# An encoder block on one core: one square moved ahead, K's low parts on GpSimd, and gate weight forms in another order

## The chip, the cores and the metric

The kernel runs on one core of one Trainium2 chip. The time is device microseconds of one execution, first to last, the lower the better. The engines are named as in the profile: PE is TensorE (matrix products), ACT is ScalarE, DVE is VectorE, POOL is GpSimd, SP is SyncE, which here issues the DMAs.

## The reference

One layer of an encoder on 1024 tokens of width 1024, all in float32:

```python
u = rms_norm(x, norm1_g)
proj = u @ w_in                       # 1024 x (3*512 + 3*512 + 2*1024)
q, k, v, cb, cc, ch, ga, gb = split(proj)
q = rms_norm(q.reshape(B, S, 8, 64), q_norm_g)
k = rms_norm(k.reshape(B, S, 8, 64), k_norm_g)
y_a = neighbourhood_attention(q, k, v, rpb) @ w_attn_branch
y_b = short_gated_conv(cb, cc, ch, conv_w) @ w_conv_branch
merged = sigmoid(ga) * y_a + sigmoid(gb) * y_b
x = x + merged @ w_o
h = rms_norm(x, norm2_g) @ w_mlp_in   # 1024 -> 4096
x = x + square(relu(h)) @ w_mlp_out
```

The attention works on a 16 x 64 grid of tokens with a window of 8 rows by 16 columns and a learned bias. The convolution has width 3.

## The kernel before

**High and low parts.** Float32 accuracy comes from 16-bit products. Each operand is scaled by a power of two and split into a high part (its rounding to float16, made by ACT) and a low part (what the rounding left out, made by DVE as value times scale minus high part). A product is three passes: high by high, high by low, low by high (`PASSES`). The scale of a weight matrix is taken from the sum of the squares of its elements: ACT squares piece after piece and adds up each row, DVE adds the pieces (L273) and puts the sum into a column of `ones` (L275), one small product on PE adds over the partitions (`all_sum`, L201), and a few short DVE instructions (L204, L435 to L442, L282) make the scale from it. Only then can ACT make the high parts of the weights (L309) and DVE the low parts (L300).

**Stages.** First the input blocks are normalised, split and transposed, and V is computed (8 blocks of 128 tokens, `v_unit`, 24 products each). Then Q (8 blocks) and K (8 blocks), 24 products each, and behind each block a chain of small steps: ACT squares the products (L747), DVE sums per head (L752), ACT takes the root (L757), DVE inverts it (L763 to L766) and multiplies (L772, and for K by the gains, L774); then ACT makes the high part (L781), DVE the low part (L786), and SP transposes the result by DMA (L793). The high and the low part of block n are put into the queues within the chain of block n + 1 (`qk_chain`). Behind K come the products of the convolution, whose weights are prepared during the K blocks, and then the attention, mixed with the rest of the convolution. Then eight gate groups, the output projection, and the MLP.

**Gates and MLP** use a scheme with seven products instead of eight for a matrix cut in 2 x 2 (`seven`). For the weights of such a group there are seven forms: the four quarters (some of them) and sums of quarters, which GpSimd makes (`gsum`, L1274). `forms_split` makes the high parts (L1294) and low parts (L1290) of the seven forms in four steps. The products of a gate group take the forms in the order 0, 5, 1, 6, 3, 4, 2, as `gate_units` gives it together with `SEVEN`. When certain steps are done, `then` counts two raw weight pieces as used up, and `load_upto` puts the loads of the next pieces into SP's queue.

**Order.** Every engine runs its queue in the order in which the program writes it. Long preparations are Python generators in the list `bg`; each `tick()` runs the first of them up to its next `yield`. During the V stage that generator is `Chunk.prep` of Q's weights: its first four steps are the four squares (L269), the next one the sum L273 and L275; the small product L201 comes once one more group of products has been written. `sform_rows(n)` scales two row blocks of the input on ACT (L491, two instructions), and `sform_sums(n)` forms four sums of them on GpSimd (L498), which the gates use much later.

Of the kernel before, what the change touches and what calls it, by code (L numbers as in the profile page):

```python
# [15 lines left out]
OP = mybir.AluOpType  # L16
# [36 lines left out]
def encoder_block(ctx: ExitStack, tc: tile.TileContext, x, weights, cols, gqk, rel, masks, out):  # L53
    nc = tc.nc
    V, A, G, T, SP = nc.vector, nc.scalar, nc.gpsimd, nc.tensor, nc.sync
# [10 lines left out]
    def bank(tag):  # L66
        return psum.tile([128, 512], F32, name="ps_" + tag, tag=tag, bufs=banks[tag])
# [29 lines left out]
    def at(c, i, n=1):  # L97
        return slice(c.start + i, c.start + i + n)
# [22 lines left out]
    def advance(g):  # L121
        try:
            return next(g) or True
        except StopIteration:
            return False
# [7 lines left out]
    def tick(n=1):  # L133

        for _ in range(n):
            i = 0
            while i < len(bg):
                r = advance(bg[i])
                if not r:
                    bg.pop(i)  # L140
                elif r == WAIT and side[0]:
                    i += 1
                else:
                    break
# [62 lines left out]
    def unit(mms, post=None, steps=0, ticks=0, free=False):  # L207

        for ps, l, r, a, b in mms:
            T.matmul(ps, l, r, start=a, stop=b, skip_group_check=free)  # L210
        for g in list(hooks):
            if not hold[0] and not advance(g):
                hooks.remove(g)
        units[0] += 1
        work[0] += len(mms) * mms[0][0].shape[-1]
        settle()
        if post:
            late.append(post)
        for i in range(max(steps, ticks)):
            if i < steps:  # L220
                step()
            if i < ticks:
                tick()
# [16 lines left out]
    def load_upto(n):  # L240
        while loaded[0] < min(n - held[0], limit[0], len(loads)):
            ch, p = loads[loaded[0]]
            loaded[0] += 1
            t = rawp.tile([128, 1024], F32, name="raw")
            load_into(t[:, :ch.widths[p][0] * ch.widths[p][1]], ch, p)
            ch.raw.append(t)
# [98 lines left out]
    for (kind, j), pieces in plan():  # L345
        ch = chunks[kind, j] = Chunk(kind, [(nk, sum(n for _, n in cs)) for _, _, nk, cs in pieces],
                                     {"A": "wa", "B": "wb"}.get(kind, "ws"), rows.get(kind, lambda j: g1)(j),
                                     j if kind == "V" else None, 9 if kind in "VQKCS" else 0)
# [8 lines left out]
    for q in range(6, 14, 2):  # L357
# [3 lines left out]
    cV, cConv, cA, cB, cO, c1, c2, c2x = ([chunks[k, j] for j in range(n)] for k, n in  # L361
                                              (("V", 2), ("C", 4), ("A", 4), ("B", 4), ("O", 2),
                                               ("1", 16), ("2", 4), ("X", 4)))
# [100 lines left out]
    def group(ps, pairs):  # L464
        return [(ps, l, r, i == 0, i == len(pairs) - 1) for i, (l, r) in enumerate(pairs)]
# [22 lines left out]
    def sform_rows(n):  # L488
        assert n in turned and n + 4 in turned
        for b in (n, n + 4):  # L490
            A.activation(xt[:, b], xt[:, b], AF.Copy, scale=sc[:, at(ys, b)])  # L491

    def sform_sums(n, part=range(4)):
        z = [xt[:, b, c:c + 512] for b in (n, n + 4) for c in (0, 512)]
        for i in part:
            o, a, b, op = ((3, 2, 3, OP.subtract), (2, 0, 2, OP.subtract),
                           (0, 3, 0, OP.subtract), (1, 1, 0, OP.add))[i]
            G.tensor_tensor(z[o], z[a], z[b], op=op)  # L498
# [29 lines left out]
    def v_unit(b, ticks):  # L528
        ps = bank("ds"[ORDER.index(b) % 2])
        order = [(k, p) for k in range(8) for p in PASSES]  # L530
        if b == 2:
            order.sort(key=lambda o: o[1] == HL)

        def post():
            hi, lo = (VT[:, b, s] for s in range(2))
            A.activation(hi, ps, AF.Copy, scale=2.0 ** -20)
            V.scalar_tensor_tensor(lo, ps, 2.0 ** -20, hi, op0=OP.mult, op1=OP.subtract)
        unit(group(ps, [(UT[:, sa, k, b * 128:(b + 1) * 128], vhome[0][:, :, sw, k * 256:(k + 1) * 256])
                        for k, (sa, sw) in order]), post, 0, ticks)
# [154 lines left out]
    settle()  # L694
    tick()
    v_unit(3, 0)
    sform_rows(3)
    sform_sums(3)
    tick(2)
    v_unit(7, 1)  # L700
    for b in 0, 1:
        ln_step(b, 2)
# [27 lines left out]
    todo = [("q", b) for b in ORDER] + [("k", b) for b in range(8)]  # L730
# [52 lines left out]
    def qk_low(n):  # L783
        d = blocks[n]
        t, q = d["t"], d["q4"]
        V.tensor_tensor(t[:, :, 1, 0], q[:, :, 0], t[:, :, 0, 0], op=OP.subtract)  # L786
        if d["r"] == 2:
            A.activation(t[:, :, 1, 1], t[:, :, 1, 0], AF.Copy)

# [5 lines left out]
    def qk_chain(n, ps):  # L795
        qk_square(n, ps)
        if n:
            qk_high(n - 1)
        qk_sum(n)
        qk_root(n)  # L800
        if n:
            qk_low(n - 1)
        qk_inverse(n)
        qk_norm(n)
# [57 lines left out]
    for half in range(2):  # L862
        unit(ch_mms(first[half], actU, half, cConv[0], 8, 384, 0), None, 8, 4)
        if half == 0:
            qk_high(15)
            qk_low(15)
            qk_turn(14)
            qk_turn(15)
# [412 lines left out]
    def parts(todo, s, then, pace=False):  # L1281

        prev = None
        for n, it in enumerate(todo + [None]):
            if prev:
                o, w = prev
                if pace:
                    yield from apart(last_low[0], 1)
                    last_low[0] = units[0]
                V.scalar_tensor_tensor(o(1), w, sc[:, s], o(0), op0=OP.mult, op1=OP.subtract)  # L1290
                then(n - 1)
            if it:
                o, w = it
                A.activation(o(0), w, AF.Copy, scale=sc[:, s])  # L1294
            prev = it
            yield

    def forms_split(ch, t, s, P):

        def then(n):  # L1300
            if n == 1 and ch is not c1[0]:
                done[0] += 2
                load_upto(done[0] + 5)
        r = ch.r
        todo = [(0, 1, r[0][:, 0:1]), (1, 3, r[1]), (3, 5, t[:, 0:2]), (5, 7, t[:, 2:4])]
        yield from parts([((lambda i, a=a, b=b: P[:, a:b, i]), w) for a, b, w in todo], s, then)

    def prep_s(n):

        ch = cS[n]  # L1310
        t = w3p.tile([128, 4, 512], F32, name="gsum", bufs=1)
        yield from rows_scaled(ch, g1)
        yield from forms_sum(ch, t, 2 - 0 * (n != 3))
        s, ch.inv = yield from scale_of(ch.sum, 9, 2 + 1*(n != 3), 0)
        hold[0] = True
        while done[0] < ch.first:
            yield WAIT
        ch.P = wsp.tile([128, 7, 2, 512], F16, name="w16_s", tag="ws")
        yield from forms_split(ch, t, s, ch.P)
        ch.split = True  # L1320
        hold[0] = False
# [320 lines left out]
    def prep1(q):  # L1642

        ch = c1[q]
        s, ch.inv = yield from scale_of(ch.sum, 9, 1)
        yield from gate(q)
        P = P1[q] = base2.tile([128, 8, 2, 512], F16, name="w16_1", tag="B")
        yield from forms_split(ch, tsum[q], s, P)
        ready.add(q)
# [712 lines left out]
```

## Time and profile before

| what | value |
|---|---|
| time, median of 3 runs | 1194.14 us (1193.83 to 1194.72) |
| profiled execution, its own time | 1194.58 us |
| its span, first to last instruction | 1192.6 us |
| granted TensorE clock | 1.00 |
| ACT busy in the span | 769.3 us (65%) |
| GpSimd busy in the span | 410.5 us (34%) |
| DMA | 189.61 MB, mean 159 GB/s |

The span is 2.0 us shorter than the execution's own time, which holds a little before the first and after the last instruction. In the timeline a line is a start, a length, an engine, a source line, an operation, output<-inputs, shapes and a count; neighbours of one kind are merged, and what stands in brackets is idle time of the engine before it and the work that ended it. In the waits a line is: who waited, for whom, us in total, times, the longest. In the view by lines, behind the bar, are the busy time, the mean ns of one, and idle time before them. In the view by windows each engine has its busy time and its number of instructions.

### The profile page before, as it was taken

The page shows a single profiled execution, that of the slowest core. Times are in us where ns is not written, and L with a number is a line of the kernel's source. Part 1 is how long each engine was busy: PE and PEld are TensorE (multiplying, and loading weights), DVE is VectorE, ACT ScalarE, POOL GpSimd, SP SyncE. Part 2 cuts the span into 40 slices and gives each one's busy share as a digit, 9 for nine tenths or more (in the row PEclk, how much of TensorE's full clock was granted, in tenths as well). Part 3 has the DMA queues.
Part 4 walks back from the last instruction along what each step waited for, and adds up shares of the span by engine and source line. Part 5 has one row for each costly group of instructions (what it writes and reads, how often), then busy time and mean ns, then how long its engine had stood idle before and what let it go on. Part 6 is the DMA issues. An engine that isn't in the chain of part 4 may idle for free.

```text
span 1192.6 us, 17069 instructions
## 1 busy us (share of the span) xinstructions
PE 1185.4 (99%) x6291; PEld 581.3 (49%) x6291; DVE 959.0 (80%) x1666; ACT 769.3 (65%) x1192; POOL 410.5 (34%) x284
## 2 busy tenths in 40 slices
PE   9999999999999999999999999999999999999998
PEld 7444445555444444444467445554444444444444
DVE  6788888899678686877886867766748899998998
ACT  7877588787667777436776576666686743646440
POOL 2640011214321212001012475776873431224194
PEclk9999999999999999999999999999999999999999
DMA  9949556776625454243374454533565927235302
GB/s 296 212 154 214 112 127 134 141 153 113 179 103 179 142 177 144 86 154 130 78 164 150 158 177 176 195 130 133 207 255 203 376 74 264 89 141 194 106 36 106
DMA packets 181283, 189.61 MB, mean 159 GB/s; under 512 B 138192, under 2 KB 138704, under 8 KB 177104
## 3 DMA queue, kind: packets, MB, share of 16 engines
q1 hardware_dynamic: 181200, 188.52, 52.4%
q8 instruction: 49, 0.80, 0.3%
q14 instruction: 34, 0.28, 0.1%
HBM read 117.19 MB, written 37.75 MB: 130 GB/s over the span
## 4 chain that ended last, share of the span: by engine, by line
PE 57%; issue 6%; POOL 5%; DMA 3%; DVE 3%; ACT 2%; SPq 0%; POOLq 0%; DVEq 0%; ACTq 0%
PE ps_s L210 21%; PE ps_d L210 20%; PE ps_o L210 15%; DMA hs<-as 3%; POOL tsum L1671 3%; POOL as L1559 2%; PE ps_d L1158 1%; DVE w L1290 1%; DVE as L2009 1%; SPq L1149 0%; ACT raw L1662 0%; DMA raw<-in_weights 0%; PE ps_o L1122 0%; ACT as L1932 0%; DVE w_s L1290 0%
## 5 line engine op out<-in xcount | busy, mean ns | idle before, releaser
L210 PEld LDWEIGHTS <-ops 128*128 128x128 f16 x1356 | 132.5, 98 | 157.3
L210 PEld LDWEIGHTS <-w 128*128 128x128 f16 x1272 | 124.4, 98 | 127.1 <-issue 0.2
L1158 PE MATMUL ps_d<-uT,w_ws 128*128 128x512 f16 x528 | 123.7, 379 | 0.0
L210 PE MATMUL ps_d<-ops 128*128 128x512 f16 (+1 forms) x528 | 119.7, 377 | 0.0
L1559 POOL TENSOR_TENSOR as<-as 128x512 f32<-128x512 f32 x56 | 92.0, 1643 | 74.0 <-ACT as L1934 71.0
L210 PE MATMUL ps_s<-ops 128*128 128x512 f16 (+1 forms) x516 | 117.1, 377 | 0.0
L2186 ACT ACTIVATE ops<-hf,sc 128x2048 f16<-128x2048 f32 x26 | 52.0, 2000 | 86.0 <-PE ps_d L210 37.5
L210 PEld LDWEIGHTS <-w_s 128*128 128x128 f16 x672 | 65.1, 98 | 79.2 <-DVE w_s L1290 1.5
L210 PEld LDWEIGHTS <-uT 128*128 128x128 f16 x528 | 51.4, 98 | 62.4 <-issue 0.6
L1671 POOL TENSOR_TENSOR tsum<-raw 128x512 f32<-128x512 f32 x28 | 40.5, 1462 | 114.4 <-ACT raw L1662 114.4
L1158 PEld LDWEIGHTS <-w_ws 128*128 128x128 f16 x528 | 51.4, 98 | 54.2
L2188 DVE SCALAR_TENSOR_TENSOR ops<-hf,sc,ops 128x2048 f16<-128x2048 f32 x26 | 69.5, 2673 | 3.5 <-ACT ops L2186 3.5
L210 PE MATMUL ps_o<-ops 128*128 128x512 f16 x312 | 71.6, 379 | 0.0
L1274 POOL TENSOR_TENSOR gsum<-raw 128x512 f32<-128x512 f32 x14 | 18.6, 1341 | 125.4 <-ACT raw L1260 100.0
L210 PE MATMUL ps_d<-u2T,w 128*128 128x512 f16 (+1 forms) x276 | 58.2, 360 | 0.0
L1290 DVE SCALAR_TENSOR_TENSOR w<-tsum,sc,w 128x1024 f16<-128x1024 f32 x28 | 46.3, 1661 | 14.5 <-ACT w L1294 14.5
L210 PE MATMUL ps_s<-u2T,w 128*128 128x512 f16 (+1 forms) x252 | 54.0, 364 | 0.0
L1290 DVE SCALAR_TENSOR_TENSOR w<-raw,sc,w 128x1024 f16<-128x1024 f32 (+1 forms) x20 | 28.2, 1417 | 31.7 <-ACT w L1294 31.7
L1932 ACT ACTIVATE as<-as 128x2048 f32<-128x2048 f32 (+1 forms) x18 | 30.9, 1718 | 31.5 <-DVE as L2009 19.3
L1088 ACT ACTIVATE sz<-sz,sc 128x384 f32<-128x384 f32 (+1 forms) x64 | 37.2, 581 | 20.9 <-DVE sc L1079 13.7
L309 ACT ACTIVATE w_ws<-raw,sc 128x512 f16<-128x512 f32 (+1 forms) x64 | 37.2, 655 | 19.6 <-DVE sc L282 19.6
L210 PE MATMUL ps_s<-u2x,w 128*128 128x512 f16 (+1 forms) x228 | 48.5, 362 | 0.0
(434 smaller groups left out, 2691.4 us busy)
## 6 DMA issues: line engine op xcount, KB each, us to landing
raw<-in_weights SPq DMA_DIRECT2D x97, 512.0 KB, 4.5
hs<-as SPq DMA_DIRECT2D x16, 1792.0 KB, 8.4
hf<-hs SPq DMA_DIRECT2D x26, 1024.0 KB, 6.0
w2x<-in_weights SPq DMA_DIRECT2D x16, 512.0 KB, 7.0
raw<-in_weights SPq DMA_DIRECT2D x16, 384.0 KB, 3.5
mL<-in_weights SPq DMA_DIRECT2D x10, 512.0 KB, 5.1
mH<-in_weights SPq DMA_DIRECT2D x9, 512.0 KB, 4.3
xt<-in_x SPq DMA_DIRECT2D x8, 512.0 KB, 7.9
```

The costliest lines, as they stand in the source:

```text
L210: T.matmul(ps, l, r, start=a, stop=b, skip_group_check=free)
L309: A.activation(self.parts[:, 0, f + o:f + o + m], self.raw[p][:, o:o + m], AF.Copy, scale=sc[:, c:c + 1])
L1088: A.activation(z, z, AF.Exp, scale=-1.0, bias=sc[:, d["mx"]], accum_out=sc[:, d["sm"]])
L1158: T.matmul(ps, l, r, start=a, stop=b)
L1274: G.tensor_tensor(t[:, o], a, b, op=OP.add)
L1290: V.scalar_tensor_tensor(o(1), w, sc[:, s], o(0), op0=OP.mult, op1=OP.subtract)
L1559: sub.tensor_tensor(z[o], z[a], z[b], op=op)
L1671: G.tensor_tensor(t[:, o], a, b, op=OP.add)
L1932: A.activation(v[:, 0:4], v[:, 0:4], AF.Relu)
L2009: add, less = (lambda o, a, b, op=op: V.tensor_tensor(o, a, b, op=op) for op in (OP.add, OP.subtract))
L2186: A.activation(P[:, 1, 0], hf, AF.Copy, scale=sc[:, Rs])
L2188: V.scalar_tensor_tensor(P[:, 1, 1], hf, sc[:, Rs], P[:, 1, 0], op0=OP.mult, op1=OP.subtract)
```

## The change

Three edits. The first moves a `tick()` of the V stage ahead of the scaling of two rows, so that the fourth square of Q's weights stands in ACT's queue before the two scalings. The second gives the low parts of K (`r` is 1) to GpSimd; those of Q stay on DVE. The third changes the order of the four steps of `forms_split`, so that the forms come as 0, 5 and 6, 1 and 2, 3 and 4, and lets `then` count the raw pieces after the third step instead of the second.

```diff
@@ -694,9 +694,10 @@
     settle()
     tick()
     v_unit(3, 0)
+    tick()
     sform_rows(3)
     sform_sums(3)
-    tick(2)
+    tick()
     v_unit(7, 1)
@@ -783,7 +784,7 @@
     def qk_low(n):
         d = blocks[n]
         t, q = d["t"], d["q4"]
-        V.tensor_tensor(t[:, :, 1, 0], q[:, :, 0], t[:, :, 0, 0], op=OP.subtract)
+        (V if d["r"] == 2 else G).tensor_tensor(t[:, :, 1, 0], q[:, :, 0], t[:, :, 0, 0], op=OP.subtract)
         if d["r"] == 2:
             A.activation(t[:, :, 1, 1], t[:, :, 1, 0], AF.Copy)
@@ -1298,11 +1299,11 @@
     def forms_split(ch, t, s, P):
 
         def then(n):
-            if n == 1 and ch is not c1[0]:
+            if n == 2 and ch is not c1[0]:
                 done[0] += 2
                 load_upto(done[0] + 5)
         r = ch.r
-        todo = [(0, 1, r[0][:, 0:1]), (1, 3, r[1]), (3, 5, t[:, 0:2]), (5, 7, t[:, 2:4])]
+        todo = [(0, 1, r[0][:, 0:1]), (5, 7, t[:, 2:4]), (1, 3, r[1]), (3, 5, t[:, 0:2])]
         yield from parts([((lambda i, a=a, b=b: P[:, a:b, i]), w) for a, b, w in todo], s, then)
```

## The prediction

> **What bounds it.** I read the page's engine times first, then the waits of PE, then the waits of all engines between 48 and 137 us, then the timeline at the three places that the change touches.
>
> ```profile
> span 1192.6 us, 17069 instructions
> ...
> PE 1185.4 (99%) x6291; PEld 581.3 (49%) x6291; DVE 959.0 (80%) x1666; ACT 769.3 (65%) x1192; POOL 410.5 (34%) x284
> ```
> ```profile
> PE ps_d L210 <- DVE w_s L1290: 0.6, 1, 0.6
> PE ps_o L201 <- DVE ones L275: 0.4, 1, 0.4
> ```
>
> TensorE is busy all but 1192.6 − 1185.4 = 7.2 us, so no edit can win more than a few us. The change aims at just two of the listed waits: 0.4 us for the sum of Q's squares (edit 1) and 0.6 us for a gate group's weight forms (edit 3). It can still lose time without limit, wherever a side chain becomes late enough to stop PE. There is one place where a side chain is already the later of the two, the start of the conv products:
>
> ```profile
> 131.59 5.34 PE L210 MATMUL ps_s<-w_ws,uT 128*128 128x512 f16 x24
> 131.85 0.60 ACT L747 ACTIVATE sq<-ps_d 128x512 f32<-128x512 f32 x1 [2.90 <-PE ps_d L210]
> ...
> 135.91 0.22 DVE L282 TENSOR_SCALAR sc<-sc 128x8 f32<-128x8 f32 x1
> 136.17 4.16 ACT L309 ACTIVATE w_ws<-raw,sc 128x384 f16<-128x384 f32 x8 [2.66 <-DVE sc L282]
> ...
> 136.84 5.57 PE L210 MATMUL ps_o<-uT,w_ws 128*128 128x512 f16 x24
> ...
> 142.25 5.34 PE L210 MATMUL ps_s<-uT,w_ws 128*128 128x512 f16 x24
> ```
>
> The last K product group starts at 131.59. A group of 24 unhindered takes about 5.18 to the next one's start (5.34 less the overlap), so PE is due at 136.77. The conv group starts at 136.84, 0.67 us after ACT begins its weights, and its successor at 142.25 where 142.02 was possible: 0.07 + 0.23 = 0.3 us are lost here, and PE follows the side chain (DVE L282, ACT L309) with no reserve. Is that side chain driven by PE, or does it run by itself?
>
> ```profile
> ACT sq L747 <- PE ps_d L210: 2.9, 1, 2.9
> ...
> ACT sq L747 <- PE ps_d L201: 1.3, 1, 1.3
> ```
>
> These are the only two entries in the waits of 48 to 137 us in which ACT, DVE or Pool waits for PE, and both belong to the last K blocks. So from 48 us until then the Q and K side chain runs by itself, behind PE, and hands on any delay.
>
> **Edit 1, the fourth square first.**
>
> ```profile
> 33.32 0.40 SPq L237 DMA_DIRECT2D raw<-in_weights  x1
> ```
> ```profile
> DMA to landing us min/median/max: 5.2/5.5/5.8
> ```
> ```profile
> 39.21 2.18 ACT L491 ACTIVATE xt<-xt,sc 128x1024 f32<-128x1024 f32 x2
> 41.29 1.04 ACT L269 ACTIVATE w_ws<-raw 128x1024 bf16<-128x1024 f32 x1
> ...
> 42.65 0.75 DVE L275 TENSOR_TENSOR ones<-sc 128x1 bf16<-128x1 f32 x1
> ...
> 43.98 4.04 DVE L456 SCALAR_TENSOR_TENSOR u<-xt,sc,u 128x1024 f16<-128x1024 f32 x2
> ...
> 48.55 0.14 DVE L204 TENSOR_SCALAR sc<-ps_o 128x1 f32<-128x1 f32 x1
> ...
> 49.74 5.01 ACT L309 ACTIVATE w_ws<-raw,sc 128x512 f16<-128x512 f32 x8 [4.27 <-DVE sc L282]
> ```
> ```profile
> 42.12 1.27 POOL L498 TENSOR_TENSOR xt<-xt 128x512 f32<-128x512 f32 x1
> ```
>
> The fourth piece of Q lands by 33.32 + 5.8 = 39.1, so the square can take ACT's place at 39.21 without a wait. The sum in `ones` (L275) is ready about 2 us earlier and PE's 0.4 us goes. The two scalings (L491) then end at 39.21 + 1.04 + 0.1 (accumulator read, an estimate) + 2.18 = 42.5, not 41.4. Pool's sums of those rows began at 42.12, as soon as Pool was free; they now begin at about 42.55, 0.4 us later. Behind them stand DVE's two L456, which take 4.04 us because Pool's sums alternate with them. So L204, and with it Q's weights (L309), move from 48.55 and 49.74 to about 48.95 and 50.15. PE needs these weights only after two more V groups, so it does not see this; the side chain does. Edit 1 by itself: 0.4 us gained on PE at 43 us, 0.4 us lost on the chain that PE meets again at 136 us.
>
> **Edit 2, K's low parts on GpSimd.** One K block's steps, the low part being L786:
>
> ```profile
> 127.93 0.68 DVE L752 TENSOR_REDUCE sc<-sq 128x8 f32<-128x512 f32 x1
> 128.05 0.63 ACT L781 ACTIVATE k<-qs 128x512 f16<-128x512 f32 x1 [0.80 <-DVE qs L774]
> 128.65 0.30 ACT L757 ACTIVATE sc<-sc 128x8 f32<-128x8 f32 x1
> 128.71 0.69 DVE L786 TENSOR_TENSOR k<-qs,k 128x512 f16<-128x512 f32 x1
> 129.32 0.19 DVE L763 RECIPROCAL sc<-sc 128x8 f32<-128x8 f32 x1
> 129.55 0.17 DVE L764 SCALAR_TENSOR_TENSOR sc<-sc 128x8 f32<-128x8 f32 x1
> 129.75 0.23 DVE L765 SCALAR_TENSOR_TENSOR sc<-sc 128x8 f32<-128x8 f32 x1
> ...
> 131.55 0.15 DVE L204 TENSOR_SCALAR sc<-ps_d 128x1 f32<-128x1 f32 x1
> ```
> ```profile
> L974 POOL TENSOR_TENSOR raw<-raw 128x512 f32<-128x512 f32 x3 | 4.0, 1336 | 15.2 <-PE ps_d L1158 15.1
> ```
> ```profile
> 64.11 3.32 POOL L498 TENSOR_TENSOR xt<-xt 128x512 f32<-128x512 f32 x1
> ...
> 66.41 1.04 DVE L102 TENSOR_TENSOR sc<-sc 128x1 f32<-128x1 f32 x1
> ```
> ```profile
> 72.12 1.30 POOL L498 TENSOR_TENSOR xt<-xt 128x512 f32<-128x512 f32 x1
> ```
> ```profile
> 72.13 0.17 DVE L764 SCALAR_TENSOR_TENSOR sc<-sc 128x8 f32<-128x8 f32 x1
> ```
>
> The block takes DVE 131.55 − 127.93 = 3.62. Without L786 the inverse waits only for the root (L757, ends 128.95), so L763 starts at 129.0 instead of 129.32: 0.3 us less, the lower bound. But the low part now starts on Pool when ACT's high part ends (128.68, Pool about 128.75) and runs 1.34 us by the mean of the 128x512 sums of L974, to 130.1. The row of L102 shows what that does to DVE: a multiplication of one column by itself took 1.04 us and ended at 67.45, with Pool's instruction (64.11 + 3.32 = 67.43). L764 is the same kind, one tile read twice from SBUF. It would start at 129.2 inside Pool's 128.75 to 130.1, end with it, and L765 follows at 130.13 instead of 129.75: +0.37 a block, the value I take. If only L765 is held, it starts inside the same instruction and ends at 130.13, not 129.98: about +0.15. The row of L764 at 72.13 (0.17, Pool's instruction only 0.01 us old) is the only one that speaks for that.
>
> The Trainium skill, SBUF — State Buffer, section "SBUF: two separate sides", says that of a VectorE op with two SBUF inputs and a GpSimd op the one that starts first has the shared ports for its whole instruction and the other blocks. By that rule L764 is held in every block, +0.37, as L102 shows and the one row of L764 does not. The GPSIMD Engine Reference, section "Engine selection", puts two-input elementwise work on GpSimd at about twice VectorE's time: an estimate of 1.38 from L786's 0.69, which would add 0.04 a block to the price from L974.
>
> Five blocks pass this way before L204 of the conv weights. In the first two, Pool's low part also stands behind a bias sum and ends some 0.1 us later still: 5 × 0.37 + 0.2 = 2.05. In the sixth, high and low parts run ahead of the root, Pool is done when L764 comes, and the missing L786 gives 0.1 back. So L282 moves by 0.4 (edit 1) + 2.05 − 0.1 = 2.35 us. The square of the sixth block waits for PE at 131.85; that reserve of DVE is nil there, since L752 follows at once. The low parts of the last two blocks run under the conv groups (5.34 us each on PE). SP's transposes of K wait for Pool instead of DVE, with only later transposes and loads behind them; attention uses the blocks in order, the last one many steps on.
>
> PE starts the conv groups at 136.84 + 2.35 = 139.2. It is due at 136.4, so it now waits 2.8 us, and edit 1's gain on PE is gone. What follows (attention, its loads) starts from there and moves as a whole.
>
> **Edit 3, forms in product order.**
>
> ```profile
> 326.22 1.28 DVE L1290 SCALAR_TENSOR_TENSOR w_s<-raw,sc,w_s 128x1024 f16<-128x1024 f32 x1
> 327.42 2.48 DVE L1290 SCALAR_TENSOR_TENSOR w_s<-gsum,sc,w_s 128x1024 f16<-128x1024 f32 x2
> ...
> 328.74 0.59 PE L210 MATMUL ps_d<-qD,w_s 128*128 128x512 f16 x2
> ...
> 329.95 2.33 PE L210 MATMUL ps_d<-qD,w_s 128*128 128x512 f16 x10 [0.62 <-DVE w_s L1290]
> ```
> ```profile
> 340.00:600.00 260.00, 260.00 (x1222) 117.89 (x1220) 204.46 (x405) 167.07 (x267) 31.97 (x24) 1.00 0.42 135
> ```
>
> The second product of group 1 needs the low part of form 5, the last of three double forms (ends 329.90). Put second it ends at 326.22 + 1.28 = 327.5, before PE asks for it at 329.3. The other two end at 328.7 and 329.9, for products that begin at 331.3 and later. The 0.62 us goes. In the later gate groups the order is free: PE is busy all 260.00 us from 340 to 600, which hides it. The raw loads come one double form (1.28 us) later in SP's queue, with nothing behind them but loads that are wanted a whole group later; that is hidden by the same PE row. With that cover gone it would cost up to 1.28 a group.
>
> **The sum.** 2.35 − 0.62 = +1.73. On the profiled execution's 1194.58 that is 1196.3; this execution lies 0.44 above the median of 1194.14, so on the median 1195.9, +0.15%. About 0.2%, 2.4 us, is what a measurement of this kernel can tell from no change, so this counts as the same.
>
> **Rivals.** (A) Pool doesn't hold DVE. Then five blocks save 0.3 each, the chain comes 1.5 − 0.4 = 1.1 earlier and is bound by PE, the 0.3 us at the conv start go too: −0.4 − 0.3 − 0.62 = −1.3, 1192.8. For it: the row of L764 alone; against: L102. (B) Slower: Pool's low parts run long. Pool's eight sums around 60 us take up to the 3.32 above. At 2.1 us instead of 1.34, five blocks add 5 × 0.76 = 3.8: 1199.7. It passes the 0.2% line from 2.4 − 1.73 = 0.7 over five blocks, a low part of 1.48 us. Against it: no DVE instruction with two SBUF inputs runs when the low part starts. (C) The new order does nothing, if PE waits for the whole weight tile: +2.35, 1196.5. Against it: PE ran two products on high parts before its wait.
>
> **Chances.** Forecast 0.56, A 0.17, B 0.14, C 0.08, 0.05 for other things. The range goes from just below A, 1192.7, to 1197.6, the forecast with 0.7 a block; B lies above it. Faster by over 0.2% needs more than A gives: 0.04. Slower by over 0.2%: B 0.14, half of C 0.04, the upper part of the forecast 0.12, together 0.30. The same: 0.66.
>
> **What would show it.** Right: no wait of L201 for L275; L204 near 48.9; K blocks 4.0 apart on DVE with L764 near 0.9; conv products starting near 139.2; no wait for L1290 near 329. Wrong: L764 at 0.17 with Pool running; a conv start at or before 136.8 (A); low parts over 1.5 us (B).

## The result, and the profile after

The changed kernel takes 1196.51 us (median of 22 executions, 1194.69 to 1198.17), the kernel before 1194.02 us (22 executions, 1193.08 to 1194.72): ratio 1.0019, 95% interval [1.0013, 1.0026]. The forecast was 1195.9. The profiled execution of the changed kernel is one of its shortest, 1194.81 us, and the reason for that turns out to be the one thing that the prediction had left out. In the changed kernel every line behind 696 has a number one higher: L786 of before is L787, L764 is L765, L1290 is L1291.

The page of the changed kernel, span and engine times:

```profile
span 1193.0 us, 17083 instructions
...
PE 1184.9 (99%) x6291; PEld 581.3 (49%) x6291; DVE 959.4 (80%) x1658; ACT 769.3 (64%) x1192; POOL 420.6 (35%) x292
```

Eight instructions went from DVE to Pool, and TensorE is idle 8.1 us instead of 7.2. The waits of PE in the changed kernel say where:

```profile
PE ps_o L210 <- ACT w_ws L309: 2.5, 1, 2.5
PE ps_s L626 <- DVE sc L379: 1.1, 1, 1.1
```

The waits for L275 and for a gate group's forms are gone; in their place PE waits 2.5 us once, for the conv weights.

The profiles begin at different moments against their first loads (the first V product stands at 22.22 us before, at 21.39 after), so moments are compared below from the first V product on; "conv +2.08" means that the conv group starts 2.08 us later than before by that count (138.08 − 21.39 against 136.84 − 22.22).

**Edit 1.** Timeline of the changed kernel at 38 to 49 us:

```profile
38.67 1.06 ACT L269 ACTIVATE w_ws<-raw 128x1024 bf16<-128x1024 f32 x1
...
39.73 2.17 ACT L491 ACTIVATE xt<-xt,sc 128x1024 f32<-128x1024 f32 x2
...
40.04 1.28 DVE L275 TENSOR_TENSOR ones<-sc 128x1 bf16<-128x1 f32 x1
...
41.97 7.04 POOL L498 TENSOR_TENSOR xt<-xt 128x512 f32<-128x512 f32 x4 [0.67 <-ACT xt L491]
42.10 0.17 PE L201 MATMUL ps_o<-ones 128*128 128x1 bf16 x1
...
43.45 4.44 DVE L456 SCALAR_TENSOR_TENSOR u<-xt,sc,u 128x1024 f16<-128x1024 f32 x2 [0.35 <-ACT u L454]
...
48.42 0.14 DVE L204 TENSOR_SCALAR sc<-ps_o 128x1 f32<-128x1 f32 x1
```

The square stands ahead of the scalings, and L201 no longer waits (it comes 0.52 us earlier). Pool now waits 0.67 us for the scalings, and L204 comes 48.42 − 21.39 against 48.55 − 22.22, 0.7 us later.

**Edit 2.** A K block of the changed kernel, and the last one ahead of the conv group:

```profile
125.11 0.68 DVE L753 TENSOR_REDUCE sc<-sq 128x8 f32<-128x512 f32 x1
125.23 0.63 ACT L782 ACTIVATE k<-qs 128x512 f16<-128x512 f32 x1 [2.52 <-DVE qs L775]
...
125.93 1.16 POOL L787 TENSOR_TENSOR k<-qs,k 128x512 f16<-128x512 f32 x1 [2.75 <-ACT k L782]
...
126.16 0.20 DVE L764 RECIPROCAL sc<-sc 128x8 f32<-128x8 f32 x1 [0.37 <-ACT sc L758]
126.39 0.72 DVE L765 SCALAR_TENSOR_TENSOR sc<-sc 128x8 f32<-128x8 f32 x1
127.15 0.23 DVE L766 SCALAR_TENSOR_TENSOR sc<-sc 128x8 f32<-128x8 f32 x1
...
129.02 0.68 DVE L753 TENSOR_REDUCE sc<-sq 128x8 f32<-128x512 f32 x1
...
135.08 0.17 DVE L765 SCALAR_TENSOR_TENSOR sc<-sc 128x8 f32<-128x8 f32 x1
...
137.15 0.22 DVE L282 TENSOR_SCALAR sc<-sc 128x8 f32<-128x8 f32 x1
...
138.08 5.58 PE L210 MATMUL ps_o<-uT,w_ws 128*128 128x512 f16 x24 [2.49 <-ACT w_ws L309]
```

Pool's low part runs from 125.93 to 127.09. L765, one column group multiplied by itself, took 0.17 us before; here it starts at 126.39 inside Pool's instruction and ends at 127.11, with it. From L753 to L753 it is 3.91 us instead of 3.62. In the last block the low part lies ahead of the root, and L765 is at 0.17 again.

**Edit 3.** The forms of gate group 1 in the changed kernel:

```profile
327.29 1.28 DVE L1291 SCALAR_TENSOR_TENSOR w_s<-gsum,sc,w_s 128x1024 f16<-128x1024 f32 x1
...
329.68 1.27 DVE L1291 SCALAR_TENSOR_TENSOR w_s<-gsum,sc,w_s 128x1024 f16<-128x1024 f32 x1
329.96 2.75 PE L210 MATMUL ps_d<-qD,w_s 128*128 128x512 f16 x12
```

The first of the three double forms (5 and 6) is ready at 328.57, and the second product group runs its twelve products without a wait.

By this profile the loss is 2.08 − 0.79 = 1.29 us at the end of the span. The medians differ by 2.49. The other 1.2 us are not in this profile.

### The profile page after: what moved, and what is told of

The parts are those of the page before. It is cut to its first block, busy times and chain, and to the rows that moved or that the text cites. A ratio compares the mean times of both kernels' runs of the same rounds, so it can differ in the third digit from the quotient of the medians.

```text
span 1193.0 us, 17083 instructions
## 1 busy us (share of the span) xinstructions
PE 1184.9 (99%) x6291; PEld 581.3 (49%) x6291; DVE 959.4 (80%) x1658; ACT 769.3 (64%) x1192; POOL 420.6 (35%) x292
## 4 chain that ended last, share of the span: by engine, by line
PE 60%; issue 6%; POOL 5%; DMA 3%; DVE 2%; ACT 1%; POOLq 0%; DVEq 0%; ACTq 0%
PE ps_s L210 22%; PE ps_d L210 21%; PE ps_o L210 15%; DMA hs<-as 3%; POOL tsum L1672 3%; POOL as L1560 2%; PE ps_d L1159 1%; DVE w L1291 1%; DVE as L2010 0%; ACT raw L1663 0%; PE ps_o L1123 0%; ACT as L1933 0%; ACT w L1295 0%; DVE tsum L1706 0%; DVE sc L320 0%
## 5 line engine op out<-in xcount | busy, mean ns | idle before, releaser
L1291 DVE SCALAR_TENSOR_TENSOR w<-tsum,sc,w 128x1024 f16<-128x1024 f32 x28 | 46.7, 1678 | 14.5 <-ACT w L1295 14.5
L1291 DVE SCALAR_TENSOR_TENSOR w<-raw,sc,w 128x1024 f16<-128x1024 f32 (+1 forms) x20 | 28.2, 1416 | 31.7 <-ACT w L1295 31.7
```

## The experiments

Times are medians. "Conv" and "end" are the start of the conv products and the end of the span in the one profile, from the first V product on, against before.

| run | what it has | time (range) | before beside it | ratio, 95% interval | conv | end |
|---|---|---|---|---|---|---|
| e1_square | edit 1 | 1194.39 (1194.12–1195.41) | 1194.15 | 1.0004 [0.9995, 1.0012] | +0.70 | +0.38 |
| e2_klow | edit 2 | 1195.56 (1195.21–1196.86) | 1194.15 | 1.0014 [1.0005, 1.0023] | +1.34 | +2.42 |
| e3_forms | edit 3 | 1193.90 (1192.88–1194.96) | 1194.15 | 0.9998 [0.9989, 1.0006] | 0.00 | −0.88 |
| e4_no_klow | edits 1, 3 | 1193.99 (1193.07–1194.37) | 1194.15 | 0.9999 [0.9990, 1.0008] | +0.47 | −0.39 |
| e0_after | all three | 1196.37 (1194.63–1197.34) | 1194.11 | 1.0017 [1.0008, 1.0026] | +1.90 | +3.04 |
| e5_twice | all, low parts doubled | 1203.48 (1202.31–1203.95) | 1194.11 | 1.0076 [1.0062, 1.0089] | +7.95 | +8.84 |
| e6_half | all, low parts halved | 1194.14 (1193.51–1195.04) | 1194.11 | 1.0001 [0.9992, 1.0010] | +0.69 | −0.04 |
| e8_forms_last | edit 3, last low parts | 1194.32 (1193.24–1195.21) | 1194.11 | 0.9999 [0.9990, 1.0007] | +0.13 | −0.22 |
| e9_fill | all, PE kept busy | 1195.41 (1194.76–1196.62) | 1194.15 | 1.0013 [1.0003, 1.0022] | +1.89 | +1.37 |
| e10_conv_first | all, conv weights earlier | 1194.80 (1193.92–1195.67) | 1194.15 | 1.0006 [0.9997, 1.0015] | −0.58 | +0.15 |
| e11_best | edits 1, 3, conv weights earlier | 1194.29 (1193.48–1195.13) | 1194.15 | 1.0001 [0.9992, 1.0010] | −0.01 | +0.45 |
| e12_scale_first | edits 1, 3, their scale earlier | 1193.50 (1192.76–1194.44) | 1194.26 | 0.9995 [0.9986, 1.0004] | −0.58 | −1.06 |

**One edit at a time.** e1_square is the first hunk of the diff alone, e2_klow the second, e3_forms the third; e4_no_klow has the first and the third.

> Edit 1 alone. Theory H (the Q and K side chain runs by itself, and Pool's instructions hold DVE's): the wait of the small product for `ones` goes, 0.4 to 0.5 us on PE, but Pool's sums and behind them L204 come 0.4 to 0.7 us later, the conv weights' L282 by as much, and PE starts the conv groups 0.4 to 0.7 us later than before: 1194.4 to 1194.7 us. Rival R (what PE wins at 43 us it keeps): 1193.5 us, conv groups 0.5 us earlier.

> Edit 2 alone. Theory H: K blocks stand 3.9 us apart on DVE instead of 3.6, L764 (now L764 as in the kernel before) 0.7 us while Pool runs, conv groups 1.5 to 1.9 us later, 1195.5 to 1196.0 us. Rival R (Pool takes work off DVE, and the loss came from the other edits): K blocks 3.3 us apart, the 0.3 us at the conv start go, 1193.7 us. Theory C, beside H (the new wait of PE also lowers the granted clock in some executions, which would explain why the changed kernel's times spread from 1194.7 to 1198.2): 1195.5 at clock 1.000 and about 1198 at 0.998.

> Edit 3 alone. Theory H and my prediction's step: the wait of 0.6 us for the last double form goes and nothing comes in its place, 1193.3 us, with a spread as small as that of the kernel before. Rival (the later loads cost what the order wins): 1194.0 us.

> Edits 1 and 3, K's low parts on DVE as before. Theory H: the conv groups start 0.4 to 0.7 us later than before and 0.7 us are won at 329 us: 1193.7 to 1194.0 us; small spread by theory C, since PE has no long wait. Rival R: both gains are kept, 1192.8 us.

The conv starts add up: 0.70 + 1.34 + 0.00 = 2.04, and all three give 2.08. Edit 1 alone moves the conv group by +0.70, edit 2 alone by +1.34, edit 3 not at all; edit 3 gives back 0.8 in the gates, in the profile of every run that has it. By its median alone (1193.90, interval on both sides of 1) e3_forms could not be told from its rival's 1194.0; it is the profile that decides there. The medians do not add up: +0.24, +1.41 and −0.25 make +1.40, where all three measured +2.49, though by their intervals each is known to about 1 us only. No edit alone has the missing 1.1 us, and edits 1 and 3 together do not have it either. The loss of clock that was looked for in e2_klow is not there: PE waits 1.2 us for the conv weights, and no execution has a mean clock under 0.999. (The profiled execution of e2_klow is the longest of its eleven; its end is not used.)

**All three again, beside other kernels.**

> The changed kernel once more, with the same runs of the kernel before as the other parts. Adding up the parts (edit 1 +0.24, edit 2 +1.41, edit 3 -0.25 by their medians on the first chip; +0.4, +2.4, -0.9 in their profiles, counted from the first V product) gives 1.4 to 1.9 us above the kernel before: about 1195.4 to 1195.9. If the three edits together also cost clock, as the spread of the first runs of the changed kernel (1194.7 to 1198.2) suggests, the median is again 2.4 us above, near 1196.5, with a spread of over 3 us. In its profile the conv products start 2.1 us later than before, counted from the first V product, by either.

It is 2.26 us again, with the wide spread. This time the profiled execution is one of the longer ones. Here are its conv group and the windows of one us around it (behind the window and its length: busy time of PE with its products, granted clock, DMA share, GB/s):

```profile
138.35 7.27 PE L210 MATMUL ps_o<-uT,w_ws 128*128 128x512 f16 x24 [2.31 <-ACT w_ws L309]
```
```profile
136.00:137.00 1.00, 0.04 (x1) 1.00 0.60 114
...
138.00:139.00 1.00, 0.61 (x2) 1.00 0.00 0
139.00:140.00 1.00, 0.99 (x3) 0.56 0.00 0
140.00:141.00 1.00, 1.00 (x3) 0.50 0.55 71
141.00:142.00 1.00, 1.00 (x4) 0.50 0.87 310
142.00:143.00 1.00, 1.00 (x5) 0.73 0.94 258
143.00:144.00 1.00, 1.00 (x7) 1.00 0.77 255
```

One row of the same view in the changed kernel's first profile, for comparison:

```profile
140.00:141.00 1.00, 1.00 (x6) 1.00 0.83 151
```

The conv group takes 7.27 us instead of 5.58. PE was idle from 136.04 to 138.35; from 139.1 to 142.5 its granted clock is 0.50, and three to five products fit into a us instead of six or seven. The loss is 0.44 + 0.50 + 0.50 + 0.27 = 1.71 us. In the first profile, after an idle time of 2.49 us, the clock stayed at 1.00 (the last section shows what differs). That is the missing part: of these eleven executions seven have a mean clock of 0.998 and take 1196.21 to 1197.34, four have 0.999 or 1.000 and take 1194.63 to 1195.29. The first 22 executions of the changed kernel divide in the same way: the ten at 0.998 have a median of 1197.19, the twelve others one of 1195.44, which is 1.4 us above the kernel before.

**Does the idle time cause it?** e9_fill keeps the late conv weights and gives PE something to do meanwhile:

```diff
     for half in range(2):
+        for i in range(9 if half == 0 else 0):
+            T.matmul(first[0], UT[:, 0, i % 8, 0:128], UT[:, 0, i % 8, 0:512], start=True, stop=True)
         unit(ch_mms(first[half], actU, half, cConv[0], 8, 384, 0), None, 8, 4)
```

> All three edits, and nine extra products (128x512, about 0.22 us each, 1.9 us in all) on TensorE between the last K group and the first conv group, into the bank that the conv group overwrites; they need nothing that is late. The two profiles of the changed kernel differ by the clock after the 2.3 to 2.5 us wait for the conv weights: 1.00 in the one, 0.50 for some 3 us in the other, whose conv group took 7.27 instead of 5.58 us. Theory C (the idle stretch itself lets the clock drop, in most executions): with 0.5 us left idle the clock stays at 1.00, the conv products start when they did, and the median falls from 1196.4 to what the starts alone give, 1195.0 to 1195.6, with a smaller spread. Rival S (the spread of the changed kernel comes from elsewhere, such as the first loads): the median stays at 1196.2 to 1196.6.

```profile
136.65 2.11 PE L865 MATMUL ps_o<-uT 128*128 128x512 f16 x9
139.12 5.58 PE L210 MATMUL ps_o<-uT,w_ws 128*128 128x512 f16 x24 [0.37 <-ACT w_ws L309]
```

The conv group starts as late as in e0_after (+1.89) and now runs at full clock: 5.58 us in the profile, a mean clock of 0.999 or 1.000 in all eleven executions where e0_after had that in four of eleven, and none above 1196.62. The median is 1195.41, as the starts alone give, 1 us under e0_after; the intervals of the two ratios overlap, and the two ran on different chips (beside the same kernel before, 1194.15 and 1194.11), so it is the clock of the executions that decides here. Kept busy with nine useless products, PE keeps its clock: the idle stretch itself costs clock, beside the time that it lasts.

**Is it Pool that holds DVE?** e5_twice lets Pool subtract each low part of K twice, e6_half lets Pool do four heads and DVE the other four.

```diff
+        if d["r"] == 1:
+            G.tensor_tensor(t[:, :, 1, 0], q[:, :, 0], t[:, :, 0, 0], op=OP.subtract)
```
```diff
-        (V if d["r"] == 2 else G).tensor_tensor(t[:, :, 1, 0], q[:, :, 0], t[:, :, 0, 0], op=OP.subtract)
+        if d["r"] == 2:
+            V.tensor_tensor(t[:, :, 1, 0], q[:, :, 0], t[:, :, 0, 0], op=OP.subtract)
+        else:
+            for e, h in ((G, slice(0, 4)), (V, slice(4, 8))):
+                e.tensor_tensor(t[:, h, 1, 0], q[:, h, 0], t[:, h, 0, 0], op=OP.subtract)
```

> The changed kernel with each low part of K subtracted twice by GpSimd, which gives the same numbers with twice the work. Theory H (GpSimd's instruction holds VectorE's multiplications of two columns groups L764/L765, and through them the whole K block): the multiplication is held until one of GpSimd's two instructions ends; the second follows the first at once and, if it gets the ports first again, holds the next one too. A K block then grows from 3.91 to between 4.2 and 5.1 us, the conv products start 1.5 to 6 us later than in the changed kernel, and the time is 1197.5 to 1202. Rival N (GpSimd only has to end before K's transposes, and the 0.3 us a block are something else, such as a semaphore from another engine): blocks stay at 3.9 us, the conv products start where they did, time as in the changed kernel, 1195.4 to 1196.5.

> All three edits, but the low part of each K block is cut in two: four heads on GpSimd, four on VectorE, at the same time. Theory H: GpSimd takes about 0.6 us and VectorE's own half, with two inputs from SBUF, is held by it or holds it, so the two run one after the other: 0.35 + 0.6 behind the high part, about as late as in the changed kernel or up to 0.2 earlier a block; block 3.7 to 3.9, conv products 1.0 to 2.1 us later than before, 1194.6 to 1196. Rival N (no hold): the low part is out of the way after 0.35 us on VectorE, the block takes 3.3 to 3.4, the conv products start with the kernel before or earlier, 1193.2 to 1194.

One block of e5_twice in the timeline (L789 is the second subtraction):

```profile
124.00 1.15 POOL L787 TENSOR_TENSOR k<-qs,k 128x512 f16<-128x512 f32 x1 [2.48 <-ACT k L782]
...
124.47 0.71 DVE L765 SCALAR_TENSOR_TENSOR sc<-sc 128x8 f32<-128x8 f32 x1
125.22 1.20 DVE L766 SCALAR_TENSOR_TENSOR sc<-sc 128x8 f32<-128x8 f32 x1
125.24 1.15 POOL L789 TENSOR_TENSOR k<-qs,k 128x512 f16<-128x512 f32 x1
...
126.72 0.69 DVE L773 TENSOR_TENSOR qs<-ps_d,sc 128x512 f32<-128x512 f32 x1
```

The first instruction of Pool ends at 125.15 and holds L765 until 125.18; the second ends at 126.39 and holds L766 (0.23 us in the changed kernel) until 126.42. A block takes 4.87 us, the conv group comes 5.9 us later than in the changed kernel, within the 1.5 to 6 expected of the hold; the rival would have left it in place. The time, 1203.48, lies above the 1202 expected, and the clock is again a part of it: PE waits 8.1 us and then runs at half clock, as the windows of this run show.

```profile
134.00:136.00 2.00, 1.80 (x9) 1.00 0.00 0
...
140.00:142.00 2.00, 0.00 (x0) 0.72 0.00 0
142.00:147.00 5.00, 3.10 (x8) 0.50 0.44 95
147.00:148.00 1.00, 1.00 (x5) 0.64 0.99 295
```

In e6_half both halves stand against each other too:

```profile
125.00 0.42 DVE L791 TENSOR_TENSOR k<-qs,k 128x256 f16<-128x256 f32 x1
125.05 0.91 POOL L791 TENSOR_TENSOR k<-qs,k 128x256 f16<-128x256 f32 x1 [2.75 <-ACT k L782]
...
125.58 0.40 DVE L765 SCALAR_TENSOR_TENSOR sc<-sc 128x8 f32<-128x8 f32 x1
```

DVE's half started first, and Pool's took 0.91 us instead of the 0.67 that it takes alone in the last block of this run; it then held L765 for 0.40. A block takes 3.66 us, close to the 3.62 of before, so the split gains nothing and loses little: conv +0.69 where edits 1 and 3 alone have +0.47. The expectation by the hold was missed on its better side (block 3.7 to 3.9, 1194.6 us or more; measured 3.66 and 1194.14), and the rival's 3.3 to 3.4 a block was not reached either.

**Low parts on Pool only at the end.** e8_forms_last has edit 3 and gives Pool just the last three low parts, two of which come after the conv group has begun.

```diff
+        (V if n < 13 else G).tensor_tensor(t[:, :, 1, 0], q[:, :, 0], t[:, :, 0, 0], op=OP.subtract)
```

> Edit 3, and K's low parts on GpSimd only for the last three K blocks, of which the root comes after the high and low parts; edit 1 is left out. Theory H: in the last blocks GpSimd's instruction lies beside ACT's root and is over, or nearly, when VectorE comes to the multiplications; VectorE is rid of two to three times 0.69 us there. The conv products start 0 to 0.3 us earlier than before, edit 3 keeps its 0.8 us, and the time is 1193.0 to 1193.9, at or a little under the kernel before. Rival N: GpSimd's low parts are late for something else in the last blocks too (transposes of K, the first attention group), so that attention starts later by up to 1 us: 1194.2 to 1195.

```profile
132.92 1.15 POOL L786 TENSOR_TENSOR k<-qs,k 128x512 f16<-128x512 f32 x1 [15.00 <-ACT k L781]
...
133.65 0.45 DVE L764 SCALAR_TENSOR_TENSOR sc<-sc 128x8 f32<-128x8 f32 x1
```

A small miss: without the delay of the earlier blocks the one low part that lies ahead of the conv group starts just before the root and not well ahead of it, and the hold is back (L764 at 0.45 until 134.10, Pool until 134.07). The conv group comes 0.13 later, not earlier. The median, 1194.32, lies in the rival's range (1194.2 to 1195), but the delay of attention that the rival named does not show: the profile loses 0.26 us in all before edit 3 wins 0.8.

**Taking the conv weights out of the way.** If everything is paid at one place, an order with a reserve there should pay it back. e10_conv_first (all edits) and e11_best (edits 1 and 3) advance the generator of the conv weights to its end before the steps of K's seventh block are written; e12_scale_first (edits 1 and 3) only by one step, so that L282 alone moves ahead of them.

```diff
-    ticks = (2, 2, 4, 4, 6, 6, 6, 6, 2, 2, 3, 4, 4, 5, 5, 1)
+    ticks = (2, 2, 4, 4, 6, 6, 6, 6, 2, 2, 3, 4, 4, 5, 11, 1)
```
```diff
-    ticks = (2, 2, 4, 4, 6, 6, 6, 6, 2, 2, 3, 4, 4, 5, 5, 1)
+    ticks = (2, 2, 4, 4, 6, 6, 6, 6, 2, 2, 3, 4, 4, 5, 6, 1)
```

> All three edits, and the generator of the conv weights advanced to its end after the unit of K's seventh block, so that L282, L309 and L300 stand ahead of the steps of the last two K blocks in the queues of VectorE and ScalarE. If the price of edits 1 and 2 is paid only because the conv weights stand behind the K blocks: PE no longer waits before the conv products, the clock stays at 1.00, and the kernel gains 2.5 us in start and its clock loss: 1192.0 to 1193.2, below the kernel before by 0.8 to 2. Rival: the last two K blocks, now some 4.5 us later on VectorE, delay the first steps of attention, which start at 146 to 148 us, by 1 to 3 us: 1193.5 to 1196.

> Edits 1 and 3 without edit 2, and the conv weights ahead of the last two K blocks as in the run with all three. Edit 1's 0.5 us at 43 us, 0.9 of the wait at the conv start and edit 3's 0.8 add up when the chain has a reserve there: 1.3 to 1.8 us below the kernel before, 1192.2 to 1192.9. If GpSimd's low parts cost nothing once the conv weights are ahead, this is within 0.4 us of the run with all three. Rival: the wait only moves to the start of attention: 1193.5 to 1195.

> Edits 1 and 3 without edit 2, and of the conv weights only the scale L282 ahead of the steps of K's seventh block; L300 keeps its place. ScalarE can then make the first high parts (L309) by about 134.5 instead of 137.1, and PE's wait of 0.9 us at the conv start goes; the first low part still stands behind the K block and ends at about 137.0, which holds the third product for about 0.3 us. The K blocks are not moved, so the sum for the first attention products is not late. Conv products start about 0.2 to 0.5 us earlier than before, counted from the first V product, instead of 0.5 later; the end comes 0.9 to 1.1 us earlier than before: 1192.9 to 1193.5. Rival: the low parts are what PE waits for, and the time stays at that of edits 1 and 3, 1193.8 to 1194.2.

In the waits of PE of e10_conv_first the rival is the first line:

```profile
PE ps_d L201 <- DVE ones L275: 1.5, 1, 1.5
```

The conv group starts 0.58 us earlier than before, but the last two K blocks, moved behind its weights, now delay L275 of the next conv weights on DVE, and with it the product L201 that stands ahead of attention. Of the 2.66 us won at the conv start 1.5 are lost again there; e11_best loses 1.3 in the same way. Both expectations (1192.0 to 1193.2 and 1192.2 to 1192.9) were missed, with 1194.80 and 1194.29 inside their rivals' ranges. e12_scale_first moves no K block, and its waits show what is left:

```profile
PE ps_o L210 <- DVE w_ws L300: 0.4, 1, 0.4
```

The 0.9 us wait of edits 1 and 3 has become 0.4 us, for the first low part, as expected; the end comes 1.06 us earlier than before, and the median is 1193.50 against 1194.26. It is the fastest kernel of this study, but the interval [0.9986, 1.0004] still holds 1: that it beats the kernel before is likely, and not shown.

## Why the prediction was right, and which step was wrong

The total was right, 1195.9 against 1196.51, and inside the range. The ratio of 1.0019 is under the 0.2% that count as the same, with its interval reaching over that line; the 2.49 us between the medians are a little over the 2.4 us that the prediction names for it. It was right with one term missing, and in part by luck.

- **Edit 1.** Right in kind: L201's wait went, PE won 0.52 us there, and the chain lost more, which PE met again at the conv start. The price was too low: L204 moved by 0.5 to 0.8 us in the profiles with edit 1 (0.70 in the first), and by 1.26 in e11_best, not by 0.4. In the first profile the two L456 begin 0.30 us later, counted from the first V product, and take 0.40 longer (4.44 instead of 4.04). How much later they begin hangs on a load that the prediction took to be in time ("so the square can take ACT's place at 39.21 without a wait"). In the first profile the fourth piece of Q lands at 38.59, which is 17.20 us after the first V product, and the square begins 0.08 us behind it; in the kernel before it landed after 16.92 us. In the five profiles with edit 1 in which it lands after 16.8 to 17.0 us, L204 moves by 0.51 to 0.54; in e11_best it lands after 17.77. L275 was held by Pool as well (1.28 us for one column, until Pool's sum ends at 41.3); that cost nothing, for PE asks at 42.10.
- **Edit 2.** Right in mechanism and place: L765 is held by Pool in five blocks and free in the sixth, 0.62 to 0.92 us where 0.9 was named. The low part takes 1.16 us, not 1.34, so a block loses 0.29 (3.91 − 3.62) and not 0.37, and e2_klow moves the conv group by 1.34, not by 1.95. With edit 1's larger price L282 moved by 2.07 where 2.35 was worked out.
- **Edit 3.** Right: the wait went, worth 0.8 us in the profiles instead of 0.62.
- **The conv start.** PE waits 2.49 us; 2.8 was forecast. Here is the step that failed: "What follows (attention, its loads) starts from there and moves as a whole." The wait was priced at its length. In 17 of 33 executions of the changed kernel (those with a mean clock of 0.998: ten of the first 22, seven of the eleven of e0_after) it costs 1.7 us more, through the clock.
- **The sum.** The terms that were priced came to +1.73 in the forecast and to 2.08 − 0.79 = 1.29 in the first profile; the clock, put at nothing, is the rest. The two errors have opposite signs, so that the total came within 0.6 us is partly luck.
- **The rivals.** A falls by every held L765. B falls by its own number, 1.16 us instead of 2.1, and C by the gate group without a wait. None of the rivals had the clock. For A the prediction named the row of L764 at 72.13 in the kernel before. The row behind it in the same timeline already spoke against A:

```profile
72.33 1.13 DVE L765 SCALAR_TENSOR_TENSOR sc<-sc 128x8 f32<-128x8 f32 x1
```

Pool's sum of 72.12 ends at 73.42 and this L765, which takes 0.23 us alone, at 73.46. Pool's instruction did hold DVE there; only L764, which started with it, came through.

The prediction took the hold from the row of L102, beside a rule that the Trainium skill gives (SBUF — State Buffer, section "SBUF: two separate sides"). The runs bear it out in both directions: DVE held by Pool, Pool held by DVE's half. On the clock the Trainium skill, TensorE: Matmul & The Clock Gate, section "🔬 Part 1: The HAM clock gate (the "warmup" mystery)", says that the array falls to half clock after an idle window of some 3.4 us, the windows running free of the program. Half clock is what the rows show (0.50). An idle time of 2.31 us was enough for it in the profile of e0_after, so a wait need not fill such a window.

## What to carry to other kernels

Work given to GpSimd is not free of VectorE: list the VectorE instructions with two SBUF inputs that fall inside each GpSimd instruction, and charge each of them to that instruction's end. A wait of TensorE costs its length only while it is short: waits of up to 1.5 us had no clock loss here, one of 2.3 to 2.5 us cost 1.7 us more in about half of the executions, so one long wait can be dearer than two short ones that lie well apart. And where a side chain arrives just in time, look for the one small instruction (here the scale L282) that can go ahead of the queue, since moving whole blocks only moved the wait to the next sum; that this makes the kernel faster than before is not shown.

## What the runs showed of the hardware

- The half clock comes in pieces of one length. In e0_after the missing 1.71 us at 0.50 are 3.42 us of half clock, which agrees with the window of some 3.4 us on the page of the Trainium skill named above; in e5_twice (2 × 0.28 + 5 × 0.50 + 0.36) / 0.50 = 6.84, twice that. In all fourteen profiles the changes of the clock (most of them behind the last products) lie on a grid of such stretches, which begins at another moment in each execution. What counts is how long PE is idle within one stretch. The first two rows are of the changed kernel's first profile, the others of e0_after:

```profile
133.72:137.13 3.41, 1.86 (x9) 1.00 0.31 58
137.13:140.55 3.42, 2.43 (x11) 1.00 0.24 41
```
```profile
135.71:139.12 3.41, 1.04 (x5) 1.00 0.41 77
139.12:142.54 3.42, 3.42 (x9) 0.50 0.56 145
```

- In the first profile the end of a stretch cuts the wait in two, 1.55 us idle in the one and 0.99 in the next, and the clock stays up. In e0_after 2.37 us idle lie in one stretch, and the whole next one runs at half clock. Over all the profiles no stretch with up to 1.68 us idle (the largest is 134.07 to 137.48 in e5_twice) brought the clock down, and every one with 2.29 us or more did (the smallest is at the end of e5_twice). So the bound lies between 1.68 and 2.29 us of idle time in one stretch. With a gap of 2.4 us that falls anywhere on the grid, between 36 and 72% of the executions would lose clock (an estimate from the two bounds); 17 of 33 did. No run was made to find the bound.
- When Pool has two instructions in a row, DVE's held one goes between them, and the next DVE instruction is held by the second (L766, 1.20 us, although its record starts 0.02 us before Pool's).
- Not held beside Pool's low parts: the inverse (L764 in the changed kernel, one input), 0.20 us in all five blocks (0.19 to 0.20 in the kernel before).
